# Both SwiGLUs of a decoder layer in two passes over their weights, with seven products of quarters for gate and linear

## The chip, the core and the metric

The kernel runs on one core of a Trainium2 chip. The metric is the device time of one launch in microseconds, from the first instruction to the last output. The engines are TensorE (PE, its weight loads PEld), VectorE (DVE), ScalarE (ACT), GpSimd (POOL) and SyncE (SP), which here only issues DMAs. Each engine takes its instructions in order.

## The reference, cut to what matters

One layer works on 1024 prompt tokens and 64 sample tokens (8 sequences of 8) with the same weights. Width is 1024, the SwiGLU's hidden width is 2816, all is float32.

```python
def swiglu(x, w_gu, w_down):
    g, u = jnp.split(x @ w_gu, 2, axis=-1)
    return (jax.nn.silu(g) * u) @ w_down

def layer(x, ...):
    h = x + 0.5 * rms_norm(swiglu(rms_norm(x, g_f1_pre), w_f1_gu, w_f1_down), g_f1_post)
    mix, k_new, v_new, s_new = mixer(rms_norm(h, g_m_pre), ...)   # attention and retention
    h = h + rms_norm(mix, g_m_post)
    h = h + 0.5 * rms_norm(swiglu(rms_norm(h, g_f2_pre), w_f2_gu, w_f2_down), g_f2_post)
    return h, k_new, v_new, s_new
```

## The kernel before

Activations stand transposed: features on the 128 partitions, tokens along the free axis. The 1088 tokens are three chunks, `CH = [(0, 384), (384, 384), (768, 320)]`.

Each float32 operand of a product is split into an upper part in fp32r (`hi`, L75, on ACT) and the rest (`lo`, L78, on DVE or POOL, source minus upper part, two SBUF tiles read). `mm3` (L85 to L92) makes a product from three matmuls: upper by upper (L87), upper by rest (L91), rest by upper (L92). Every matmul has a weight load of its own.

A SwiGLU (`ffn`, L317) walks over the 22 blocks f of 128 hidden columns, two at a time. For each f it loads the gate block and the linear block (8 tiles of 128x128 each, 512 KB) and the down block (512 KB), and splits each (`unit`: tiles wr, wh, wl, whd, wld). For each chunk, `gu` makes the gate product (8 `mm3`), a Silu on ACT (L337), the linear product (8 `mm3`), their product on DVE (L342, tile fs), and its two parts hh and hl. `down` (L349) multiplies these by the two down blocks for 8 blocks of output, and DVE adds each into the tile y (L359). So weights are read once and all tokens go by them; all 1088 tokens of a SwiGLU have ended before the boundary behind it is done.

A boundary (L283) is the post-norm, the residual and the next pre-norm: squares on ACT (L241) summed on DVE (L243), a small chain for the reciprocal root, then 8 steps with the gain (L294, one operand in PSUM), the residual from DRAM (xr, L296, half on POOL, half on DVE), the same squares again and L305. The three chunks take turns in `BOUNDARY_ORDER`. The layer starts with `first_norm` (L184), chunk by chunk among the first products, and ends with `stages_last`.

A scheduler sets each engine's order from program order and dependencies; pools give tiles with a number of buffers, and a tile's next user waits until its last reader is done. PSUM has two banks pa, two pb, three pc and one pm.

Of the kernel before, what the change touches and what calls it, by code (L numbers as in the profile page):

```python
# [2 lines left out]

# [14 lines left out]
P = 128  # L18
# [27 lines left out]
FIRST_HEAD = 7  # L46
BOUNDARY_ORDER = (0, 0, 1, 0, 1, 2, 1, 2, 2)


class Trunk:  # L50
# [11 lines left out]
    def pool(self, name, ctx=None, **kw):  # L62
        kw.setdefault("bufs", 1)
        return (ctx or self.ctx).enter_context(self.tc.tile_pool(name=name, **kw))
# [20 lines left out]
    def mm3(self, ps, wh, wl, xh, xl, first, last):  # L85
        mm = self.nc.tensor.matmul
        ins = mm(ps, wh, xh, start=first, stop=False)  # L87
        if self.pin is not None:
            self.behind(ins, self.pin)
            self.pin = None  # L90
        mm(ps, wh, xl, start=False, stop=False)  # L91
        mm(ps, wl, xh, start=False, stop=last)  # L92

    def unit(self, src, pool=None, sfx="", eng=None):
# [3 lines left out]
        raw = self.t(self.wraw, [P, 1024], "wr", bufs=2)  # L98
# [24 lines left out]
    def setup(self):  # L123
# [3 lines left out]
        self.wsp = self.pool("wsp", bufs=4)  # L127
        self.up = self.pool("up")
        self.gstage = self.pool("gst")
# [17 lines left out]
        self.mrT = self.t(self.dram, [D, T], "mrT")  # L147

# [9 lines left out]
    def rows_of_pages(self):  # L158
# [3 lines left out]
        t = self.t(self.gstage, [P, 384], "gs", bufs=3)  # L162
# [21 lines left out]
    def first_norm(self, pl, u, y, c):  # L184

        nc = self.nc
        co, cn = CH[c]
        out = self.bank("pb")
        dg = self.t(pl, [P, 3, P], "ndg", bufs=2)
        ss = self.t(pl, [P, 3], "ss", bufs=2)  # L190
        nc.gpsimd.memset(ss, 1.0)
        for j in range(3):
            o, n = TOK[3 * c + j]
            xn = self.t(pl, [P, D], "xn", bufs=3)
            nc.sync.dma_start(xn[:n], self.rows(3 * c + j))
            sq = self.t(pl, [P, D], "xsq")
            ins = nc.scalar.activation(sq[:n], xn[:n], AF.Square, accum_out=ss[:n, j : j + 1])
            if c == 1:
                self.behind(ins, self.first[1])
            for q in range(2):  # L200
                ps = self.bank("pc")
                for k in range(4):
                    ins = nc.tensor.transpose(ps[:, k * P : k * P + n],
                                              xn[:n, (4 * q + k) * P : (4 * q + k + 1) * P], self.ident[:n, :n])
                    if c == 1:
                        self.behind(ins, self.first[0])
                pv = ps.rearrange("p (k c) -> p k c", c=P)[:, :, :n]
                yv = y[:, 4 * q : 4 * q + 4, o - co : o - co + n]
                if c == 0:
                    nc.vector.tensor_copy(yv, pv)  # L210
                else:
                    nc.scalar.activation(yv, pv, AF.Copy)
        nc.vector.tensor_scalar(ss, ss, 1.0 / D, EPS, op0=ALU.mult, op1=ALU.add)
        nc.vector.reciprocal(ss, ss)
        nc.scalar.activation(ss, ss, AF.Sqrt)
        for j in range(3):
            o, n = TOK[3 * c + j]
            nc.vector.tensor_scalar(dg[:n, j, :n], self.ident[:n, :n], ss[:n, j : j + 1], None, op0=ALU.mult)
            ins = nc.tensor.matmul(out[:, o - co : o - co + n], self.ones[:n, :], dg[:n, j, :n], start=True, stop=True)
        if c == 0:  # L220
            self.first = [ins.ins]
            self.gains(["g_ffn1_pre"])
        g = self.gain["g_ffn1_pre"]
        for d in range(KD):
            v = self.t(pl, [P, 384], "nu", bufs=2)
# [1127 lines left out]
```

## Time and profile before

| | us |
|---|---|
| median of 3 runs | 3019.94 (3017.34 to 3020.51) |
| the profiled execution | 3022.61 |
| its span | 3020.7 |
| granted TensorE clock, mean | 0.989 |
| PE busy / DVE / ACT / POOL | 2943.9 / 1571.7 / 1066.9 / 305.7 |

A span is what the profile covers; the execution has 1.9 us around it. A matmul's busy time overlaps the next one's, so TensorE's load is read from distances between starts. Roughly, the first SwiGLU fills the span up to 800 us, its boundary follows until 900, the mixer reaches to about 2150, and the second SwiGLU to the end.

### The profile page before, as it was taken

Reading aid. Unit: us, or ns where it says so; the run is one execution under the profiler, and the core shown is the slowest. Engines: PE = TensorE matmul, PEld = TensorE weight load, DVE = VectorE, ACT = ScalarE, POOL = GpSimd, SP = SyncE. Lnnn points to the kernel's source line nnn. Section 1 sums busy time; section 2 is a strip of 40 time slices with the busy share of each in tenths; the row PEclk is TensorE's granted clock in tenths of the full one; section 3 lists DMA queues with packets and bytes.
Section 4 is the critical chain, followed back from the end, with each engine's and each line's share of the span. In section 5 each row is a group of like instructions: output and inputs, shape, how many; then the busy total and the mean of one; then the engine's idle time right before and its main releaser. Section 6 shows DMA issues by size and latency. Waiting matters only on the chain.

```text
span 3020.7 us, 44684 instructions
## 1 busy us (share of the span) xinstructions
PE 2943.9 (97%) x17944; PEld 2857.6 (95%) x17944; DVE 1571.7 (52%) x3034; ACT 1066.9 (35%) x2027; POOL 305.7 (10%) x339
## 2 busy tenths in 40 slices
PE   8999999999989999999999989999999999999998
PEld 7999999999989999989999878879999999999998
DVE  4333333333753554448888578876463333333336
ACT  5211111111443343336666577753342111111113
POOL 1000000000330000000000345430230000000001
PEclk9999999999999999999999999999999999999999
DMA  5211111111242332233223577767242111111112
GB/s 160 82 50 49 43 43 42 43 42 43 84 152 61 93 105 81 85 95 81 68 64 90 184 246 267 262 199 228 74 124 67 43 42 43 42 43 43 42 43 94
DMA packets 289200, 282.40 MB, mean 93 GB/s; under 512 B 25121, under 2 KB 263585, under 8 KB 288993
## 3 DMA queue, kind: packets, MB, share of 16 engines
q1 hardware_dynamic: 266720, 208.23, 22.4%
q0 software_dynamic: 22272, 71.31, 7.2%
q8 instruction: 141, 2.31, 0.3%
q14 instruction: 67, 0.54, 0.1%
HBM read 223.79 MB, written 51.51 MB: 91 GB/s over the span
## 4 chain that ended last, share of the span: by engine, by line
PE 61%; DVE 5%; DMA 2%; issue 1%; ACT 1%; POOL 0%; SPq 0%; DVEq 0%; ACTq 0%; POOLq 0%
PE pa L87 13%; PE pa L92 13%; PE pa L91 13%; PE pc L87 3%; PE pc L92 3%; PE pc L91 3%; PE pb L802 2%; PE pc L828 2%; PE pb L87 1%; PE pb L92 1%; PE pb L91 1%; DMA ul<-orT 1%; PE pm L631 1%; PE pm L855 1%; PE pm L856 1%
## 5 line engine op out<-in xcount | busy, mean ns | idle before, releaser
L87 PE MATMUL pa<-uh,wh 128*128 128x384 f32 (+1 forms) x3552 | 1171.8, 331 | 11.8 <-ACT gs L406 5.6
L92 PE MATMUL pa<-uh,wl 128*128 128x384 f32 (+1 forms) x3552 | 1166.8, 329 | 0.0
L91 PE MATMUL pa<-ul,wh 128*128 128x384 f32 (+1 forms) x3552 | 1165.8, 328 | 0.5 <-POOL ul L78 0.4
L87 PEld LDWEIGHTS pa<-uh,wh 128*128 128x128 f32 x3552 | 670.6, 189 | 23.5 <-ACT gs L406 6.7
L91 PEld LDWEIGHTS pa<-ul,wh 128*128 128x128 f32 x3552 | 670.4, 189 | 6.9 <-POOL ul L78 1.2
L92 PEld LDWEIGHTS pa<-uh,wl 128*128 128x128 f32 x3552 | 670.1, 189 | 3.0 <-issue 1.2
L359 DVE TENSOR_TENSOR y<-y,pc 128x384 f32<-128x384 f32 (+1 forms) x480 | 253.8, 531 | 417.7 <-PE pc L92 417.3
L91 PE MATMUL pc<-hl,whd 128*128 128x384 f32 (+1 forms) x1056 | 345.3, 327 | 0.8 <-DVE hl L78 0.8
L87 PE MATMUL pc<-hh,whd 128*128 128x384 f32 (+1 forms) x1056 | 342.9, 328 | 1.8 <-DVE y L359 1.7
L92 PE MATMUL pc<-hh,wld 128*128 128x384 f32 (+1 forms) x1056 | 342.1, 327 | 0.0
L78 DVE TENSOR_TENSOR wl<-wr,wh 128x1024 fp32r<-128x1024 f32 x144 | 176.2, 1224 | 212.6 <-ACT wh L75 198.9
L75 ACT ACTIVATE wh<-wr 128x1024 fp32r<-128x1024 f32 x156 | 165.4, 1060 | 291.9 <-PE pa L91 243.4
L342 DVE TENSOR_TENSOR fs<-fs,pa 128x384 f32<-128x384 f32 x132 | 69.9, 530 | 314.2 <-PE pa L92 312.3
L337 ACT ACTIVATE fs<-pa 128x384 f32<-128x384 f32 x132 | 61.8, 468 | 453.3 <-PE pa L92 453.2
L75 ACT ACTIVATE hh<-fs 128x384 fp32r<-128x384 f32 x132 | 66.2, 501 | 420.5 <-DVE fs L342 420.4
L87 PEld LDWEIGHTS pc<-hh,whd 128*128 128x128 f32 x1056 | 198.4, 188 | 2.4 <-DVE y L359 2.2
L91 PEld LDWEIGHTS pc<-hl,whd 128*128 128x128 f32 x1056 | 199.0, 188 | 1.2 <-DVE hl L78 1.2
L92 PEld LDWEIGHTS pc<-hh,wld 128*128 128x128 f32 x1056 | 198.9, 189 | 0.0
L296 POOL TENSOR_TENSOR y<-y,xr 128x384 f32<-128x384 f32 (+1 forms) x24 | 29.2, 1223 | 857.0 <-DVE y L294 839.7
L78 DVE TENSOR_TENSOR ktl<-pc,kth 128x512 fp32r<-128x512 f32 x128 | 86.4, 684 | 20.5 <-ACT kth L75 19.5
L669 DVE TENSOR_TENSOR_SCAN pt<-pt 128x129 f32<-128x129 f32 (+3 forms) x96 | 91.6, 956 | 6.5 <-ACT pt L660 2.0
L78 DVE TENSOR_TENSOR hl<-fs,hh 128x384 fp32r<-128x384 f32 x132 | 72.8, 552 | 35.8 <-ACT hh L75 35.6
(308 smaller groups left out, 3786.3 us busy)
## 6 DMA issues: line engine op xcount, KB each, us to landing
wr<-in_w_ffn_gu_dram SPq DMA_DIRECT2D x88, 512.0 KB
wr<-in_w_in_dram SPq DMA_DIRECT2D x52, 512.0 KB
wr<-in_w_ffn_down_dram SPq DMA_DIRECT2D x44, 512.0 KB
xn<-in_x_prompt_dram SPq DMA_DIRECT2D x8, 512.0 KB
s<-in_state_ret_dram SPq DMA_DIRECT2D x16, 256.0 KB
rgs<-grT SPq DMA_DIRECT2D x16, 256.0 KB
ut_ret_state_sample_dram<-s SPq DMA_DIRECT2D x16, 256.0 KB
orT<-oc SPq DMA_DIRECT2D x16, 256.0 KB
```

The lines of the kernel that those rows point to most:

```text
L75: return self.nc.scalar.activation(dst, src, AF.Copy)
L78: (eng or self.nc.vector).tensor_tensor(dst, src, hi.bitcast(F32), op=ALU.subtract)
L87: ins = mm(ps, wh, xh, start=first, stop=False)
L91: mm(ps, wh, xl, start=False, stop=False)
L92: mm(ps, wl, xh, start=False, stop=last)
L337: nc.scalar.activation(s[:, :n], pg[:, :n], AF.Silu)
L342: nc.vector.tensor_tensor(h[:, :n], s[:, :n], pu[:, :n], op=ALU.mult)
L359: nc.vector.tensor_tensor(y[c][:, d, :n], y[c][:, d, :n], ps[:, :n], op=ALU.add)
L631: ins = nc.tensor.matmul(po[:, lo:256], vs[:, j, :], ats[j // 4][x][:, j % 4, lo:256], start=(j == 0 and x == 0), stop=(j == last and x == 1))
L669: nc.vector.tensor_tensor_scan(rev, rev, rev, initial=1.0, op0=ALU.mult, op1=ALU.bypass)
L802: ins = nc.tensor.matmul(ps, qd[:, b2, m * P : (m + 1) * P], kt, start=(m == 0 and x == 0), stop=(m == 3 and x == 1))
L828: nc.tensor.transpose(tp[:, i * P : (i + 1) * P], kp[i // 2][:, (i % 2) * 512 + m * P : (i % 2) * 512 + (m + 1) * P], self.ident)
```

## The change

Tokens go through a SwiGLU in two passes, 512 in pass 0 and 576 in pass 1 (`PASSES` holds the start and half the width: 256 and 288). A pass reads all weights again. The products of a block f are a 2x2 scheme: the rows are gate and linear block, the inner dimension is halved (features 0 to 511 and 512 to 1023), the columns are the two halves of the pass's tokens. Seven products of quarters (4 `mm3` each, of 256 or 288 columns) take the place of eight, in Winograd's form of Strassen's scheme. For this the weights need four sums (POOL, L464, L465, L466, L471 of the kernel after) and seven splits of 512 (sh, sl) instead of two of 1024. The tokens' quarters need four sums per block of features (`sums`), which are made once a pass. The results take three additions on DVE with a PSUM operand, two on POOL (L507, L508), and products accumulate in a PSUM bank that ACT has meanwhile read out.

```diff
+PASSES = ((0, 256), (512, 288))
+B11, B21, B22, T1, T2, T3, T4 = range(7)
+USED = (B11, T2, T3, T1, B21, T4, B22)
...
+    def sums(self, pl, q11, q12, q21, q22, emit, eng=None):
+        tt = (eng or self.nc.gpsimd).tensor_tensor
...
+        emit(B11, q11)
+        tt(t1, q12, q11, op=ALU.subtract)
+        tt(t2, q22, t1, op=ALU.subtract)
+        emit(T2, t2)
+        tt(q12, q22, q12, op=ALU.subtract)
+        emit(T3, q12)
+        emit(T1, t1)
+        emit(B21, q21)
+        tt(t4, q21, t2, op=ALU.subtract)
+        emit(T4, t4)
+        emit(B22, q22)
...
+    def late_quarters(self, u):
+        for b in USED:
+            lf = u[1][b].bitcast(F32)
+            self.nc.sync.dma_start(lf, self.cB[:, b])
+            self.hi(u[0][b], lf)
+            self.lo(u[1][b], lf, u[0][b])
...
+    def swiglu_weights(self, wgu, f):
...
+        names = ("A11", "S2", "S3", "S1", "A12", "A22", "S4")
+        out = {x: [self.t(self.sw, [P, 512], y, F32R, bufs=9) for y in ("sh", "sl")] for x in names}
...
+        tt = nc.gpsimd.tensor_tensor
+        split("A11", g0)
+        split("A22", v1)
+        tt(v1, v0, v1, op=ALU.add)
+        tt(v0, g0, v0, op=ALU.subtract)
+        tt(g0, v1, g0, op=ALU.subtract)
+        split("S2", g0)
+        split("S3", v0)
+        split("S1", v1)
+        split("A12", g1)
+        tt(g1, g1, g0, op=ALU.subtract)
+        split("S4", g1)
+        return out
+
+    def swiglu_hidden(self, w, u, n):
...
+        px = self.bank("pa")
+        product(px, "A11", B11)
+        p1 = kept("p1", px)
+        py = self.bank("pb")
+        product(py, "S2", T2)
+        u2 = self.t(fs, [P, 288], "u2", bufs=2)[:, :n]
+        tt(u2, py[:, :n], p1, op=ALU.add)
+        pw = self.bank("pa")
+        product(pw, "S3", T3)
+        p7 = kept("p7", pw)
+        pz = self.bank("pb")
+        product(pz, "S1", T1)
+        p5 = kept("p5", pz)
+        nc.gpsimd.tensor_tensor(p7, p7, p5, op=ALU.add)
+        nc.gpsimd.tensor_tensor(p7, p7, u2, op=ALU.add)
+        product(px, "A12", B21, True)
+        nc.scalar.activation(h1, px[:, :n], AF.Silu)
+        product(pw, "A22", T4, True)
+        c21 = self.t(fs, [P, 288], "c21")[:, :n]
+        tt(c21, pw[:, :n], u2, op=ALU.add)
+        tt(h1, h1, c21, op=ALU.mult)
+        product(pz, "S4", B22, True)
+        tt(h2, pz[:, :n], u2, op=ALU.add)
+        nc.scalar.activation(h2, h2, AF.Silu)
+        tt(h2, h2, p7, op=ALU.mult)
...
+            for p, (o, n) in enumerate(PASSES):
+                for g in range(0, NF, 2):
+                    hid = [self.swiglu_hidden(self.swiglu_weights(wgu, f), q, n) for f in (g, g + 1)]
...
+                    if g + 2 == NF and p == 0:
+                        q = self.new_quarters(self.qpool, PASSES[1][1])
+                        self.late_quarters(q)
+                    down(p, g, dw, hid)
+                    side(p, g // 2)
...
-                for c, (o, n) in enumerate(CH):
+                for c, (o, n) in enumerate(mch):
```

In `down`, a chunk is 512 wide in pass 0; in pass 1 it is 256 and 320 (first SwiGLU) or 320 and 256 (second). What lies around the SwiGLUs moves too. `first_norm` now covers the first 512 tokens; the others are normed beside pass 0 (`second_norm`), and their quarters go to DRAM (cB) and come back between the passes (`late_quarters`). The boundary of pass 0's tokens runs beside pass 1, in halves of 256; behind the first SwiGLU only 576 tokens are left (256 and 320), and the normed first 512 come back from DRAM (unT). The output products of the mixer go in chunks of 512, 288 and 288 (`mch`); the first 512 tokens' boundary and quarters come before the second SwiGLU, the others' beside its pass 0. Pools of SBUF get `reuse_waits="tile"`.

Three places in the engines' order follow. In the kernel after, `hi` is L88, `lo` L91, `mm3` L100 to L105, and the addition into y L570.

TensorE in the middle of the first SwiGLU before: the down products (pc) of a pair stand between the gate and linear products (pa) of the next.

```order
L92 MATMUL pc_2568<-hh_2402,wld_2175 128x384
L87 MATMUL pa_2749<-uh_13_92,wh_2720 128x384
L91 MATMUL pa_2749<-ul_16_95,wh_2720 128x384
L92 MATMUL pa_2749<-uh_13_92,wl_2721 128x384
L87 MATMUL pa_2749<-uh_13_92,wh_2720 128x384
L87 MATMUL pc_2576<-hh_2231,whd_2168 128x384
L91 MATMUL pc_2576<-hl_2232,whd_2168 128x384
L92 MATMUL pc_2576<-hh_2231,wld_2169 128x384
```

TensorE in pass 0 after, at the same place: pa_1578 is A22's product, pb_1709 the next f's S2, pb_1593 S4's product.

```order
L105 MATMUL pa_1578<-q_22_107,sl_1526 128x256
L100 MATMUL pb_1709<-q_18_103,sh_1663 128x256
L100 MATMUL pc_1454<-hh_1268,whd_1420 128x512
L104 MATMUL pc_1454<-hl_1269,whd_1420 128x512
L105 MATMUL pc_1454<-hh_1268,wld_1421 128x512
L100 MATMUL pc_1454<-hh_1414,whd_1426 128x512
L104 MATMUL pc_1454<-hl_1415,whd_1426 128x512
L105 MATMUL pc_1454<-hh_1414,wld_1427 128x512
L100 MATMUL pb_1593<-q_23_108,sh_1527 128x256
```

The down products stand between quarters' products of 12 matmuls as before, now 512 wide, and a product of the next f can be begun ahead.

POOL before, from the end of the start to the first SwiGLU's boundary: nothing stands between the last lower part of the start and the first residual.

```order
L78 TENSOR_TENSOR ul_18_97<-nu_725,uh_15_94 128x320
L78 TENSOR_TENSOR ul_18_97<-nu_729,uh_15_94 128x320
L296 TENSOR_TENSOR y_19_110<-y_19_110,xr_6746 128x384
L296 TENSOR_TENSOR y_19_110<-y_19_110,xr_6755 128x384
L296 TENSOR_TENSOR y_19_110<-y_19_110,xr_6764 128x384
```

POOL after, for one f in pass 0: wr are the raw weights, p and u the kept results.

```order
L464 TENSOR_TENSOR wr_444_2282<-wr_444_2282 128x512
L465 TENSOR_TENSOR wr_444_2282<-wr_2281,wr_444_2282 128x512
L466 TENSOR_TENSOR wr_2281<-wr_444_2282,wr_2281 128x512
L507 TENSOR_TENSOR p_420_2122<-p_420_2122,p_422_2137 128x256
L508 TENSOR_TENSOR p_420_2122<-p_420_2122,u_418_2107 128x256
L471 TENSOR_TENSOR wr_2281<-wr_2281 128x512
```

Six sums for each f are new on POOL, all from SBUF.

DVE before, in the same SwiGLU: additions into y, with one product and one lower part of the hidden block among them.

```order
L359 TENSOR_TENSOR y_20_114<-y_20_114,pc_4318 128x384
L342 TENSOR_TENSOR fs_4484<-fs_4484,pa_4459 128x384
L359 TENSOR_TENSOR y_20_114<-y_20_114,pc_4326 128x384
L78 TENSOR_TENSOR hl_4512<-fs_4484,hh_4511 128x384
L359 TENSOR_TENSOR y_20_114<-y_20_114,pc_4334 128x384
```

DVE after, in pass 0: sl are lower parts of the quarters of the next f, hf the hidden block.

```order
L515 TENSOR_TENSOR c_350_1781<-pa_1724,u_345_1722 128x256
L516 TENSOR_TENSOR hf_1693<-hf_1693,c_350_1781 128x256
L91 TENSOR_TENSOR sl_1913<-wr_1896,sh_1912 128x512
L91 TENSOR_TENSOR sl_2047<-wr_2042,sh_2046 128x512
L519 TENSOR_TENSOR hf_1693<-pb_1739,u_345_1722 128x256
L91 TENSOR_TENSOR sl_2057<-wr_399_2043,sh_2056 128x512
L521 TENSOR_TENSOR hf_1693<-hf_1693,p_347_1737 128x256
L91 TENSOR_TENSOR hl_1800<-hf_1693,hh_1799 128x512
L499 TENSOR_TENSOR u_390_1961<-pb_1948,p_388_1946 128x256
L91 TENSOR_TENSOR sl_2049<-wr_2042,sh_2048 128x512
```

Between the steps of the hidden block now stand lower parts of weights; the next f's A11 (sl_2047) and A22 (sl_2057) come before S2 (sl_2049), which needs POOL's three sums.

580 lines of the change are left out of this document (364 added, 216 removed).

## The prediction

> **What bounds the kernel now.** I read the page's busy line and chain first, then the stages, then the shapes of each engine, then single rows where two engines meet.
>
> ```profile
> span 3020.7 us, 44684 instructions
> PE 2943.9 (97%) x17944; PEld 2857.6 (95%) x17944; DVE 1571.7 (52%) x3034; ACT 1066.9 (35%) x2027; POOL 305.7 (10%) x339
> PE 61%; DVE 5%; DMA 2%; issue 1%; ACT 1%; POOL 0%; SPq 0%; DVEq 0%; ACTq 0%; POOLq 0%
> ```
>
> TensorE carries the chain. The stages (the columns are the window, its length, busy time of PE, PEld, DVE, ACT and POOL with counts, granted clock, DMA share, GB/s) show where it does not:
>
> ```profile
> 0.00:75.00 75.00, 62.35 (x340) 59.69 (x341) 37.52 (x76) 42.97 (x71) 9.44 (x19) 0.91 0.53 159
> 300.00:500.00 200.00, 200.00 (x1213) 200.00 (x1212) 71.28 (x117) 31.73 (x49) 0.00 (x0) 1.00 0.14 43
> 800.00:850.00 50.00, 43.02 (x254) 41.46 (x253) 42.04 (x87) 25.66 (x51) 22.12 (x16) 0.92 0.49 158
> 850.00:900.00 50.00, 44.49 (x236) 42.64 (x236) 22.80 (x43) 21.96 (x40) 20.11 (x24) 0.87 0.40 127
> 3000.00:3021.00 21.00, 10.38 (x64) 8.64 (x63) 11.81 (x25) 8.78 (x19) 2.87 (x2) 0.81 0.61 217
> ```
>
> In the middle of a SwiGLU TensorE never rests, DVE is busy 36%, ACT 16%, POOL not at all: time there is the sum of the spacings of matmuls. A row's own duration (0.28 to 0.40 us) overlaps the next, so I take start to start. First and last of a run, the columns being start and duration: 24 of 320 columns, 51 of 384, twelve of 256, three of 512.
>
> ```profile
> 409.44 0.31 PE L87 MATMUL pa<-uh,wh 128*128 128x320 f32 x1
> 412.81 0.31 PE L92 MATMUL pa<-uh,wl 128*128 128x320 f32 x1
> ...
> 413.31 0.34 PE L87 MATMUL pa<-uh,wh 128*128 128x384 f32 x1
> 421.98 0.33 PE L92 MATMUL pa<-uh,wl 128*128 128x384 f32 x1
> ...
> 971.96 0.28 PE L91 MATMUL pb<-rscl,rvh 128*128 128x256 f32 x1
> 973.27 0.28 PE L92 MATMUL pm<-rvh,kdl 128*128 128x256 f32 x1
> ...
> 2006.33 0.40 PE L856 MATMUL pm<-vl,at 128*128 128x512 f32 x1
> 2006.79 0.46 PE L856 MATMUL pm<-vl,at 128*128 128x512 f32 x1
> ```
>
> That gives 0.1465, 0.1734, 0.119 and 0.23 us. 288 columns lie halfway between 256 and 320: 0.1328. Check: a mix of two 384s and one 320 is 0.1644, and 200 us over 1213 is 0.1649.
>
> **The change: TensorE.** I count by pair of column blocks f, which is the kernel's unit (11 pairs in a SwiGLU). Before, a pair has 144 matmuls for each of three chunks: 288 x 0.1734 + 144 x 0.1465 = 71.0 us. After, pass 0 has 2 x 84 at 256 and 48 down matmuls at 512: 20.0 + 11.0 = 31.0. Pass 1 has 168 at 288 and 48 each at 256 and 320: 22.3 + 12.7 = 35.0. So 66.1 against 71.0, 4.95 less for a pair, 109 us for 22 pairs. One eighth of the gate and linear products goes, but narrower matmuls give back half of it, since their fixed part is some 0.01 us each. The Trainium skill (TensorE: Matmul & The Clock Gate, "Wait — 56ns, not 53.3ns?") puts spacing at columns over 2.4 GHz plus 2.5 ns; estimated by that the saving would be 117, and the rows, with a larger fixed part, contradict it.
>
> **What stands beside it: DVE and POOL.** These engines now split seven weight quarters for each f and pass instead of two blocks once, and POOL makes four sums of weights and two of results. Durations:
>
> ```profile
> L78 DVE TENSOR_TENSOR wl<-wr,wh 128x1024 fp32r<-128x1024 f32 x144 | 176.2, 1224 | 212.6 <-ACT wh L75 198.9 <-PE pc L1051 13.5
> L78 DVE TENSOR_TENSOR ktl<-pc,kth 128x512 fp32r<-128x512 f32 x128 | 86.4, 684 | 20.5 <-ACT kth L75 19.5
> L243 DVE TENSOR_TENSOR acc<-acc,sq 128x256 f32<-128x256 f32 x16 | 6.6, 415 | 0.1
> L75 ACT ACTIVATE vh<-wl 128x512 fp32r<-128x512 f32 x64 | 39.7, 627 | 21.1 <-PE pm L855 13.3 <-DMA wl<-in_cache_v_dram,rowix 2.8 <-DVE pt L748 2.0
> ...
> 809.06 0.55 DVE L243 TENSOR_TENSOR accb<-accb,sqb 128x384 f32<-128x384 f32 x1
> 809.53 0.54 DVE L359 TENSOR_TENSOR y<-y,pc 128x384 f32<-128x384 f32 x1
> ...
> 822.83 8.22 POOL L78 TENSOR_TENSOR ul<-y,uh 128x384 fp32r<-128x384 f32 x8 [5.60 <-ACT uh L75]
> ```
>
> Back to back, DVE instructions start 0.08 us sooner than the one before ends (0.47 for 0.55), so one of 1024 costs 1.14, of 512 0.60, of 256 0.335; by the line through these, of 288 0.37 and of 576 0.67. A pair of pass 0 needs 14 lower parts of 512, two of the hidden block, two of down weights, four products from SBUF (13.2 us), and six evacuations of 256 and eight additions of 512 into y (6.8): 20.0 us of 31.0. Pass 1: 13.5 + 8.1 = 21.6 of 35.0. ACT has 16 of 512, two of 1024 (twice that) and ten of 256 (at most half): about 16 us. POOL takes 1.03 us for 384 and 2.36 for 1024 (below), so 1.30 for 512, 0.76 for 256, 0.83 for 288: 13.4 us a pair in pass 0, 13.7 in pass 1. Taken singly, all are hidden under TensorE. Together they are not free:
>
> ```profile
> 795.99 2.81 POOL L78 TENSOR_TENSOR wl<-wr,wh 128x1024 fp32r<-128x1024 f32 x1
> ...
> 796.45 0.55 DVE L359 TENSOR_TENSOR y<-y,pc 128x384 f32<-128x384 f32 x1
> 796.92 2.31 DVE L296 TENSOR_TENSOR y<-y,xr 128x384 f32<-128x384 f32 x1
> ...
> 814.87 2.36 POOL L78 TENSOR_TENSOR wl<-wr,wh 128x1024 fp32r<-128x1024 f32 x1 [3.00 <-ACT wh L75]
> ...
> 815.36 2.21 DVE L78 TENSOR_TENSOR hl<-fs,hh 128x320 fp32r<-128x320 f32 x1 [0.26 <-ACT hh L75]
> ```
>
> A DVE instruction that reads two SBUF tiles (hl, y with xr) lasts until POOL's has ended, 2.2 us instead of 0.5, while one with a PSUM operand beside the same POOL instruction keeps its 0.55. The Trainium skill (SBUF — State Buffer, "Who interferes with whom") says just this, an exclusive lock on a shared read port. By its rule 13.2 + 13.4 = 26.6 us of a 31.0 us pair hold the lock, which alone would stall nothing.
>
> But both engines take their instructions in order, and one chain has little slack. When TensorE has used S1 of the pair's second f, the slot for the next f's A22 is free. Then follow ACT's upper part (0.6), DVE's lower part, three POOL sums one after another, ACT and DVE again for S2: 0.6 + 0.6 + 3.9 + 0.6 + 0.6 = 6.3, with six handovers some 6.9 us. TensorE's order gives it three products, the next A11 and about nine down matmuls: 48 x 0.119 + 9 x 0.23 = 7.8 us. With the lock, two DVE instructions of 0.6 slip between the POOL sums and one DVE part waits for half a sum (0.65): 8.8. The slot opens once a pair, so I add 1.3 us a pair, rounded up for the additions into y that queue behind a blocked part: 44 pairs, +57 us. The ends: 0, if collisions fall into slack, and 176 us (second rival). Gaps of 1 us cost no clock as yet; a longer one does:
>
> ```profile
> 33.71 0.69 PE L87 MATMUL pa<-uh,wh 128*128 128x384 f32 x1 [2.47 <-ACT fs L337]
> 34.20 0.52 PE L91 MATMUL pa<-ul,wh 128*128 128x384 f32 x1
> 34.52 0.52 PE L92 MATMUL pa<-uh,wl 128*128 128x384 f32 x1
> ```
>
> After 2.47 us of idleness the spacing is 0.32 instead of 0.17.
>
> Added weight loads (66 of 512 KB in a SwiGLU) double a DMA share of 0.14; SP issues them in program order, between the boundaries' loads and spills, and each has a 15 us f to land in. I add nothing; without that cover a late load would stop the chain above at its first split.
>
> **The seams.** Start: the second 256 tokens need 16 POOL sums (12.2 us) beside six of weights (7.8) before all quarters stand, while TensorE has two f's products with B11 and B21 to do; the window from 0 to 75 loses 12.7 us as it is. +5 (-5 to +15). End of the first SwiGLU: 800 to 900 loses 12.5 us idle and some 9 to the clock; 512 of 1088 tokens now go through it under pass 1: -8 (-18 to +5). Into the second SwiGLU: 512 tokens' norms (36 additions and 32 gains of 256, some 25 us of DVE), their quarters (5 + 9) and a pair's weights (8) make 48 on DVE, two thirds of POOL's 16 on top, 59, against 16 x 24 x 0.1328 = 51 us of output products: +8, and +4 for the two norm chains: +12 (0 to +30). Between passes the late quarters are seven splits of 1152 (1.27 each, 9 us) on a DVE two thirds full: +4 twice (0 to +16). Tail: -3 (-8 to +3). The mixer's own work is the same. Sum +14, ends about -10 and +45.
>
> **Sum.** The profiled execution took 3022.6 us, the span and 1.9 around it, 2.7 above the median of 3019.9. 3022.6 - 109 + 57 + 14 = 2984.6; against the median, 2982.
>
> **Rivals.**
> First, all hidden: the lock's collisions stay in slack. For it: 26.6 of 31.0, and two products of lead in the weight slots (nine, seven used). Against: the chain above. Time: 2982 - 57 = 2925, with good seams 2905.
> Second, slower: DVE becomes the bound. If every microsecond of POOL stops it, a pair of pass 0 takes 33.4 and one of pass 1 35.3; the work beside (second norm, 23 us of DVE and POOL over 11 pairs; boundaries with quarters, 40; boundaries of pass 1, 29) adds 2.1, 3.6 and 2.4. That is 5.3 over TensorE in pass 0 and 2.7 in pass 1, 176 us: 3101, with partial overlap some 3060. Against: a third of DVE's time reads PSUM and passes. It decides from (109 - 14) / 44 = 2.2 us a pair.
> Third, the change does not save TensorE time: weight loads bind at 256 columns. Their mean is 189 ns, above the 119 spacing:
>
> ```profile
> L87 PEld LDWEIGHTS pa<-uh,wh 128*128 128x128 f32 x3552 | 670.6, 189 | 23.5 <-ACT gs L406 6.7 <-ACT fs L337 3.8 <-ACT qdec L540 2.7
> ```
>
> But the 256-column run above has a load for each matmul and kept 0.119, so loads overlap. At 0.146 as for 320, pass 0 and pass 1 would lose 22 x (168 x 0.027 + 168 x 0.0137) = 150 us, and the time be 3130.
>
> **How the numbers follow.** Forecast 0.45, its own range 2940 to 3015; hidden 0.25; DVE bound 0.26; no saving 0.04. Within 0.2% (6 us, about what a measurement of this kernel can tell from no change) lies the forecast's upper edge: 0.07. Faster: 0.25 and most of 0.45, 0.66. Slower: 0.27. The range of eight in ten reaches from the hidden case with good seams, 2905, into the DVE case, 3070.
>
> **What will show it.** Right: 256- and 288-column matmuls at 0.119 and 0.133 start to start; POOL at some 13 us a pair; lower parts of 512 with a mean of 0.8 to 1.0 us where undisturbed ones take 0.68; TensorE idle about 1 us a pair, released by ACT or DVE with S2's parts. Wrong: idle before down matmuls released by DVE's additions into y, or a granted clock below 0.95 in the SwiGLUs (DVE bound); TensorE without gaps (hidden); spacing above 0.13 at 256 (no saving). The seams may also cost more than 30 us where output products run out.

## The result and the profile after

| | us | against the kernel before, same chip |
|---|---|---|
| before, median of 4 runs | 3020.2 (3017.3 to 3022.3) | |
| after, median of 4 runs | 3043.5 (3041.2 to 3050.7) | 1.0082 (1.0063 to 1.0101) |
| forecast | 2982 (2905 to 3070) | |

The changed kernel is 0.8% slower, a small step but clear of the spread of the runs. The time lies in the forecast's range, on the other side of the kernel before.

The page of the kernel after, its span, the busy line and the chain of work:

```profile
span 3042.1 us, 50675 instructions
...
PE 2875.8 (95%) x19002; PEld 2715.4 (89%) x19002; DVE 2212.6 (73%) x4059; ACT 1480.9 (49%) x2953; POOL 1004.9 (33%) x879
...
PE 16%; DVE 5%; POOL 2%; issue 2%; DMA 1%; ACT 1%; SPq 0%; POOLq 0%; DVEq 0%; ACTq 0%
```

The shares of the chain (16% for TensorE, 61% before) cannot be compared: they are shares of the whole span, and here the chain could be followed back only to 2242 us, before to 888. What changed is read from the stages. Those of the kernel after (columns as in the prediction: the window, its length, PE, PEld, DVE, ACT and POOL with counts, granted clock, DMA share, GB/s) follow:

```profile
0.00:75.00 75.00, 48.13 (x244) 42.13 (x245) 55.11 (x97) 43.71 (x99) 33.35 (x41) 0.91 0.57 152
150.00:240.00 90.00, 90.00 (x635) 83.92 (x634) 73.40 (x113) 46.66 (x90) 45.51 (x34) 1.00 0.45 137
400.00:530.00 130.00, 118.45 (x816) 111.58 (x815) 123.59 (x221) 71.84 (x139) 61.12 (x48) 0.99 0.44 133
600.00:760.00 160.00, 160.00 (x1206) 160.00 (x1205) 116.19 (x205) 65.82 (x124) 71.14 (x54) 1.00 0.29 87
800.00:850.00 50.00, 39.97 (x233) 38.24 (x232) 38.84 (x73) 29.65 (x53) 17.07 (x14) 0.87 0.52 155
850.00:900.00 50.00, 40.82 (x223) 39.46 (x223) 21.81 (x44) 19.73 (x35) 15.37 (x20) 0.85 0.42 133
2200.00:2275.00 75.00, 52.90 (x346) 49.05 (x346) 61.51 (x131) 39.51 (x96) 33.13 (x21) 0.84 0.40 120
```

The second and the fourth row are pairs with no other work beside them, in pass 0 and pass 1: TensorE rests nowhere, though DVE is busy 82% and 73%. The others are the start, the change of passes with the first boundary beside it (DVE 95%), the end of the first SwiGLU, and the way into the second. Two runs of products in clean pairs of the kernel after, 33 matmuls of 256 columns and twelve of 288 (start and duration, first and last of each):

```profile
159.79 0.28 PE L100 MATMUL pa<-q,sh 128*128 128x256 f32 x1
163.56 0.27 PE L105 MATMUL pa<-q,sl 128*128 128x256 f32 x1
...
650.13 0.29 PE L100 MATMUL pa<-q,sh 128*128 128x288 f32 x1
651.60 0.29 PE L105 MATMUL pa<-q,sl 128*128 128x288 f32 x1
```

3.77 us over 32 is 0.118, 1.47 over 11 is 0.1336: the spacings of the forecast. So I can work out for every stage what TensorE lost beyond its spacing: the distances between neighbouring starts, each less the spacing of its width (0.119, 0.1328, 0.1465, 0.1734 and 0.23 us; 0.11 for narrower ones). Stages are the first 100 us; from there to the last down product of the first SwiGLU; the 80 us behind it; the mixer; the two output products; 60 us behind them; the rest of the second SwiGLU; the last 5 us of down products and all that follows. Each kernel's profiled execution, in us:

| | start | first SwiGLU | behind it | mixer | output products | into the second | second SwiGLU | tail | sum |
|---|---|---|---|---|---|---|---|---|---|
| before | 18.6 | 8.0 | 18.0 | 89.9 | 5.3 | 2.8 | 1.5 | 5.5 | 149.6 |
| after | 41.0 | 37.2 | 21.6 | 95.3 | 9.5 | 31.7 | 32.4 | 8.9 | 277.6 |
| difference | +22.4 | +29.2 | +3.6 | +5.4 | +4.2 | +28.9 | +30.9 | +3.4 | +128.0 |

Span less loss is TensorE's own work: 2871.1 before, 2764.5 after, 106.6 less where the forecast had 109. The saving is all there; 128 us of new waiting ate it. Of the 60 us that the two SwiGLUs lose more, some 53 stand at 240 to 300 us (7.9, second norm's last part), 400 to 530 (19.1), 2300 to 2400 (12.6, the boundary beside pass 0) and 2575 to 2700 (14.1), all with work beside the pair, and most of the rest at 3000 to 3013, where the last pair ends. The clean pairs of the table's second and fourth row lose 0.3 and 0.1 us.

What holds TensorE up on the way into the second SwiGLU (the two longest waits of PE in 2200 to 2275: in total, times, longest):

```profile
PE pm L382 <- DVE acc L371: 5.8, 1, 5.8
PE pb L100 <- ACT sh L88: 5.3, 1, 5.3
```

Inside that gap stand these instructions of DVE and POOL (start, duration):

```profile
2223.64 0.68 DVE L91 TENSOR_TENSOR sl<-wr,sh 128x512 fp32r<-128x512 f32 x1
...
2224.45 6.52 POOL L464 TENSOR_TENSOR wr<-wr 128x512 f32<-128x512 f32 x1 [20.99 <-DVE sl L91]
...
2224.91 1.21 DVE L91 TENSOR_TENSOR wld<-wrd,whd 128x1024 fp32r<-128x1024 f32 x1
...
2227.05 0.45 DVE L371 TENSOR_TENSOR acc<-acc,sq 128x288 f32<-128x288 f32 x1
...
2231.05 1.26 POOL L465 TENSOR_TENSOR wr<-wr,wr 128x512 f32<-128x512 f32 x1
```

The first sum of weights, 1.26 us of work by the row below it, takes 6.52 on POOL: DVE streams instructions with two SBUF operands without a break until 2229.8, and POOL gets through only behind them. S2 (a sum of weight quarters) waits for that sum and the two behind it, and TensorE for S2: the 5.3 us. The 5.8 us before are a small matmul of the boundary of the last 576 tokens, whose sum of squares (2227.05) stands in the same stream of DVE. At the change of passes the hold goes the other way (DVE's groups in 400 to 530: busy, mean ns, idle before):

```profile
L371 DVE TENSOR_TENSOR acc<-acc,sq 128x256 f32<-128x256 f32 x28 | 21.3, 762 | 0.4
...
L91 DVE TENSOR_TENSOR q<-q,q 128x1152 fp32r<-128x1152 f32 x5 | 9.6, 1929 | 0.0
```

A sum of squares of 256 takes 0.76 us, undisturbed 0.42. All 28 sums of the boundary stand in these 130 us, just where the late quarters are split.

### The profile page after: what moved, and what is told of

Read it like the earlier page. It is cut to its first block, busy times and chain, and to the rows that moved or that the text cites. A ratio compares the mean times of both kernels' runs of the same rounds, so it can differ in the third digit from the quotient of the medians.

```text
span 3042.1 us, 50675 instructions
## 1 busy us (share of the span) xinstructions
PE 2875.8 (95%) x19002; PEld 2715.4 (89%) x19002; DVE 2212.6 (73%) x4059; ACT 1480.9 (49%) x2953; POOL 1004.9 (33%) x879
## 5 line engine op out<-in xcount | busy, mean ns | idle before, releaser
L88 ACT ACTIVATE sh<-wr 128x512 fp32r<-128x512 f32 x616 | 351.8, 622 | 411.3 <-POOL wr L471 192.8
L91 DVE TENSOR_TENSOR sl<-wr,sh 128x512 fp32r<-128x512 f32 x616 | 443.3, 746 | 116.5 <-ACT sh L88 115.0
L100 PE MATMUL pa<-uh,wh 128*128 128x384 f32 (+1 forms) x1440 | 483.4, 336 | 7.5 <-ACT gs L598 2.5
L105 PE MATMUL pa<-uh,wl 128*128 128x384 f32 (+1 forms) x1440 | 477.0, 331 | 0.0
L104 PE MATMUL pa<-ul,wh 128*128 128x384 f32 (+1 forms) x1440 | 476.7, 331 | 0.0
L100 PE MATMUL pa<-q,sh 128*128 128x256 f32 (+1 forms) x1408 | 411.2, 292 | 11.0 <-DVE c L515 5.4
L104 PE MATMUL pa<-q,sh 128*128 128x256 f32 (+1 forms) x1408 | 411.3, 292 | 6.0 <-DVE q L91 5.9
L105 PE MATMUL pa<-q,sl 128*128 128x256 f32 (+1 forms) x1408 | 409.4, 291 | 0.7 <-DVE sl L91 0.7
L100 PE MATMUL pc<-hh,whd 128*128 128x256 f32 (+2 forms) x1056 | 329.2, 333 | 19.7 <-ACT hh L88 14.7
L105 PE MATMUL pc<-hh,wld 128*128 128x256 f32 (+2 forms) x1056 | 344.2, 329 | 0.0
L100 PE MATMUL pb<-q,sh 128*128 128x288 f32 (+1 forms) x1056 | 308.4, 293 | 16.5 <-ACT sh L88 9.5
L104 PE MATMUL pb<-q,sh 128*128 128x288 f32 (+1 forms) x1056 | 309.2, 293 | 5.5 <-DVE q L91 5.5
L570 DVE TENSOR_TENSOR y<-y,pc 128x512 f32<-128x512 f32 (+2 forms) x480 | 243.9, 525 | 89.9 <-PE pc L105 88.2
L105 PE MATMUL pb<-q,sl 128*128 128x288 f32 (+1 forms) x1056 | 308.1, 292 | 0.4 <-DVE sl L91 0.3
L100 PEld LDWEIGHTS pa<-uh,wh 128*128 128x128 f32 x1440 | 274.4, 191 | 18.2 <-ACT uh L88 2.9
L100 PEld LDWEIGHTS pa<-q,sh 128*128 128x128 f32 x1408 | 269.1, 191 | 18.0 <-DVE c L515 6.4
L104 PEld LDWEIGHTS pa<-q,sh 128*128 128x128 f32 x1408 | 268.8, 191 | 11.2 <-DVE q L91 8.4
L105 PEld LDWEIGHTS pa<-uh,wl 128*128 128x128 f32 x1440 | 273.8, 190 | 2.9 <-issue 1.2
L105 PEld LDWEIGHTS pa<-q,sl 128*128 128x128 f32 x1408 | 268.6, 191 | 2.6 <-DVE sl L91 0.9
L464 POOL TENSOR_TENSOR wr<-wr 128x512 f32<-128x512 f32 x88 | 129.2, 1468 | 359.2 <-DVE sl L91 343.0
```

What stands on the lines that cost most here:

```text
L88: return self.nc.scalar.activation(dst, src, AF.Copy)
L91: (eng or self.nc.vector).tensor_tensor(dst, src, hi.bitcast(F32), op=ALU.subtract)
L464: tt(v1, v0, v1, op=ALU.add)
L570: nc.vector.tensor_tensor(y[p][:, d, c], y[p][:, d, c], ps[:, :n], op=ALU.add)
```

## The experiments

Theory: TensorE's new waits lie where other work stands beside the pairs, because DVE is full there, and it is full for two reasons: POOL's sums hold it up (and it them), and the side work is crowded into short stretches. Rivals: plain load (DVE would be full without POOL's help at any order), the boundaries alone, the layout in two passes. Each ratio is against runs of the kernel before on the same chip.

**Sums on DVE** (the edit at the weights; `sums` and the two sums of results likewise).

```diff
-        tt = nc.gpsimd.tensor_tensor
+        tt = nc.vector.tensor_tensor
```

> All sums of weights, of results and of the tokens' quarters go from POOL to DVE (the splits stay where they are). Theory of the lock: the 130 us that TensorE loses beyond its spacing in the stretches with side work (start, 240 to 300 us, both pass changes, into the second SwiGLU) come from DVE and POOL holding each other up; a POOL sum of 512 takes 1.3 to 1.45 us and now and then 3 to 6, DVE does it in 0.60. So TensorE's idle time falls in all these stretches, start -8 to -10, into the second SwiGLU -10 to -15, each pass change -6, 2300 to 2400 -8: 2990 to 3005 us, DVE's lower parts of 512 back to a mean of 0.69. Rival, plain load: DVE is simply full there, and POOL carries 6.2 us a pair for it at a cost of 3.4 us of stretching; then the clean passes stay hidden (26 of 31 and 28 of 35 us), but the 15 or so pairs with side work lose 2.8 us more each and the start 8: about 3090 us.

Measured: 3022.3 us, 0.9996 (0.9985 to 1.0006): 21 us faster than after, about half of what the theory of the lock said, and far from 3090. The page, two groups of it, and three windows:

```profile
PE 2865.4 (95%) x19002; PEld 2713.3 (90%) x19002; DVE 2304.1 (76%) x4635; ACT 1486.7 (49%) x2953; POOL 260.1 (9%) x303
```

```profile
L91 DVE TENSOR_TENSOR sl<-wr,sh 128x512 fp32r<-128x512 f32 x616 | 404.1, 685 | 33.0 <-ACT sh L88 31.2
L464 DVE TENSOR_TENSOR wr<-wr 128x512 f32<-128x512 f32 x88 | 60.5, 687 | 0.2
```

```profile
0.00:75.00 75.00, 48.43 (x291) 44.20 (x292) 60.51 (x144) 47.95 (x107) 1.06 (x11) 0.82 0.61 163
400.00:530.00 130.00, 125.27 (x898) 122.76 (x898) 123.15 (x270) 72.22 (x142) 8.04 (x8) 0.97 0.44 130
2200.00:2275.00 75.00, 53.35 (x356) 49.56 (x355) 71.75 (x170) 45.18 (x103) 3.51 (x4) 0.82 0.44 133
```

745 us of POOL's busy time are gone and DVE has 92 more: the sums take some 290 us there (0.69 each for 512 columns), but DVE's other work takes some 200 less. Which instructions got shorter tells why. These are two groups of the kernel after and the same two of this run:

```profile
L516 DVE TENSOR_TENSOR hf<-hf,c 128x256 f32<-128x256 f32 (+1 forms) x88 | 69.9, 794 | 4.9 <-ACT hf L511 0.7
L515 DVE TENSOR_TENSOR c<-pa,u 128x256 f32<-128x256 f32 (+1 forms) x88 | 38.0, 431 | 17.1 <-PE pa L105 17.0
...
L516 DVE TENSOR_TENSOR hf<-hf,c 128x256 f32<-128x256 f32 (+1 forms) x88 | 39.4, 447 | 1.5 <-ACT hf L511 0.6
L515 DVE TENSOR_TENSOR c<-pa,u 128x256 f32<-128x256 f32 (+1 forms) x88 | 38.2, 434 | 9.5 <-PE pa L105 9.1
```

The product of two SBUF tiles goes from 794 to 447 ns and the lower parts of weights from 746 to 685; the addition of the same width with an operand in PSUM stays as it was (431 and 434). The start loses 33.2 in place of 41.0, the change of passes 9.3 in place of 19.1; the way into the second SwiGLU hardly changes (29.0 for 31.7), and DVE is still 95% busy in both of the later windows. So the lock was one cause, and not the only one.

**Side work in fine steps**, alone and with the sums on DVE.

```diff
+                        tick(p, g // 2)       # behind each block of down products: one step
...
-                    next(todo["ends"][BOUNDARY_ORDER[g - 1]], None)
+        todo["t1", 1] = ticker([fine(0, o, 256, ...) for o in (0, 256)], 1, 3)
```

> The work beside the passes (second norm, boundaries, quarters, last boundary of the first 512 tokens) is cut into steps of one or two DVE instructions and handed out one at a time behind each block of down products (every one in pass 0, every third in pass 1), in place of lumps of 8 to 15 us once a pair. Sums stay on POOL. Theory that lumps cause the loss inside the passes: 240 to 300 (7.9 us), 2300 to 2400 (12.5) and two thirds of the pass changes (19 and 14) go: about -35, 3005 to 3015 us, with the start and the way into the second SwiGLU unchanged. Rival, DVE has too little time for side work at any spacing (21 us of pair plus 3.5 of stretching plus side work): 3035 to 3050.

> Both edits together: sums on DVE and side work in fine steps. If lock and lumps are separate causes, the gains add, 2955 to 2975 us, faster than the kernel before. If spreading works only because it keeps DVE from being full for long, sums on DVE give part of it back: 2985 to 3005. If plain load rules: above 3040.

Measured: 3039.3 us, 1.0055 (1.0042 to 1.0069), and 3025.3 us, 1.0005 (0.9996 to 1.0014): next to nothing by itself, nothing on top of the sums. DVE's sums of squares in 400 to 530 of the run with sums on POOL show why:

```profile
L457 DVE TENSOR_TENSOR acc<-acc,sq 128x256 f32<-128x256 f32 x28 | 20.5, 732 | 0.2
```

All 28 still stand in that window, though the program now hands them out over eight pairs. The order is the scheduler's, which put the finer steps back to the same place. For the boundaries this run tested nothing of the theory; the order had to be pinned. Only at 240 to 300 us, beside the second norm, did the loss fall, from 7.9 to 0.8 us.

**Boundaries beside the passes left out.**

```diff
-                todo["ends"] = [first_boundary(0, o, 256, kept, ("pm", "pm")) for o in (0, 256)]
+                todo["ends"] = [self.bare(y[0][:, :, o : o + 256], o, 256, self.h1T, kept) for o in (0, 256)]
```

> Left out: the boundary of the first 512 tokens beside pass 1 of the first SwiGLU and that of the last 576 beside pass 0 of the second (only their copies to DRAM stay). That takes some 42 and 47 us of DVE off the stretches 400 to 530 and 2260 to 2400. Theory that the boundaries fill DVE there: TensorE's loss falls from 19 to about 8 at the first pass change and from 12.5 to 1 in 2300 to 2400, some of the 7 us behind the start of the second SwiGLU too: -25 to -30, 3013 to 3018 us. Rival, late quarters are what TensorE waits for at the pass change: only -12 to -15, 3030.

Measured: 3009.0 us, 0.9951 (0.9937 to 0.9964), 34 less than after, a little more than the theory's 25 to 30. The window of the change of passes:

```profile
400.00:530.00 130.00, 127.97 (x924) 125.04 (x925) 104.68 (x164) 56.96 (x107) 61.26 (x45) 1.00 0.41 126
```

TensorE loses 3.5 us there in place of 19.1, with the late quarters still in it, and 0.4 in place of 12.6 at 2300 to 2400. It is the boundary, or rather its meeting with the late quarters, not the quarters alone.

**Output products in smaller chunks** (with the sums on DVE).

```diff
-        mch = [(0, 512), (512, 288), (800, 288)]
+        mch = [(0, 256), (256, 256), (512, 288), (800, 288)]
```

> Sums on DVE as in the first run, and the mixer's output products in chunks of 256, 256, 288, 288 in place of 512, 288, 288: the first half of the first 512 tokens is done some 22 us sooner. Theory of the chain: TensorE's 30 us of loss on the way into the second SwiGLU come from two post-norms and two pre-norms one after another (squares, root, gains, residuals) that begin too late, with DVE only half busy: beginning 22 us sooner takes 12 to 18 us off, 3004 to 3010 us. Rival: the amount of DVE work just ahead of the first products (quarters, 28 lower parts, weights of two f) sets it: 0 to 4 us off, 3018 to 3022.

Measured: 3035.0 us, 1.0037 (1.0024 to 1.0050), 13 slower than with the sums on DVE alone. Both theories are wrong here, the first most. The longest wait of PE in 2180 to 2300, and from the same trace what stands before S2:

```profile
PE pb L100 <- ACT sh L88: 15.2, 2, 12.6
```

```profile
2232.14 0.68 DVE L464 TENSOR_TENSOR wr<-wr 128x512 f32<-128x512 f32 x1
2233.08 3.47 DVE L422 SCALAR_TENSOR_TENSOR y<-y,g_mix_post,pm 128x288 f32<-128x288 f32 x8
...
2239.56 0.67 DVE L466 TENSOR_TENSOR wr<-wr,wr 128x512 f32<-128x512 f32 x1
2242.30 0.44 ACT L369 ACTIVATE acc<-y 128x288 f32<-128x288 f32 x1 [3.68 <-POOL y L424]
2242.64 2.18 ACT L88 ACTIVATE sh<-wr 128x512 fp32r<-128x512 f32 x4
```

The output products lost 18.6 us in place of 10.1, and TensorE still stood 12.6 us before S2. Beginning the norms sooner did not bring the first pair's weights forward: between the first (L464) and the last (L466) of the three sums, 8.1 us, DVE has eight gains of the next tokens' boundary (3.47 us), quarters and down weights, and then S2's upper part stands 2.4 us behind a square on ACT that waits for that boundary's residual on POOL. Why the output products lose 8.5 us more stays open.

**Seven slots in place of nine for weight quarters.**

```diff
-        out = {x: [self.t(self.sw, [P, 512], y, F32R, bufs=9) for y in ("sh", "sl")] for x in names}
+        out = {x: [self.t(self.sw, [P, 512], y, F32R, bufs=7) for y in ("sh", "sl")] for x in names}
```

> Slots for weight quarters cut from nine to seven, so that A22 of the next f can only be split when TensorE has used this f's A22. Theory: the two slots of lead are what hid the chain that the prediction charged with 1.3 us a pair; without them the chain (8 to 9 us) has only S4's and A11's products beside it (2.9 us) at every f that no down products follow, 4 to 6 us of idle time at each of 44 places: 3220 to 3300 us. Rival, TensorE's order finds other work: within 20 us of 3043.

Measured: 3042.4 us, 1.0063 (1.0042 to 1.0083): as after. My reading of the slots fell. From the trace, the time between the end of a quarter's lower part on DVE and the first product that reads it, in clean pairs of pass 1 (600 to 760 us), median of nine f (A22 is a quarter as loaded; S2, S3 and S1 are made by POOL's three sums):

| | A22 | S2 | S3 | S1 |
|---|---|---|---|---|
| after | 27.5 | 9.8 | 13.6 | 14.0 |
| seven slots | 24.8 | 5.7 | 9.0 | 12.3 |

A22 is split more than 20 us ahead of its product either way, while by a strict turn of seven slots it could not be split before this f's A22 had been used, 12 to 21 us ahead of the next. The slots are thus not handed out in the fixed turn on which the prediction's chain rested. The addresses of the tiles in the built program show the turn: in the kernel after, the lower part of A22 takes over the slot of S4 of two f before in 75 of 88 cases, not that of S1 of the f before. In the trace (600 to 760 us) its split on DVE starts 1 to 4 us after that slot's last use, so it does wait for a slot, but for one that comes free early.

**Eight products in the same two passes.**

```diff
-USED = (B11, T2, T3, T1, B21, T4, B22)
+USED = (B11, B21, B12, B22)
...
-        names = ("A11", "S2", "S3", "S1", "A12", "A22", "S4")
+        names = ("A11", "A12", "A21", "A22")
```

> The two passes without Strassen's scheme: eight products of quarters of the same widths, weights split into four quarters of 512, no sums of weights, tokens or results. TensorE's work by the spacings is 133 us more than with seven, 24 more than in the kernel before. Theory that seven splits and the sums cause what TensorE lost inside the passes and at the pass changes, and the layout causes the rest (later start, way into the second SwiGLU, mixer): 3085 to 3105 us, seven products thus worth only some 50 of 133. Rival, the two-pass layout loses all of the 130 us: 3170.

Measured: 3067.2 us, 1.0145 (1.0124 to 1.0166), less than both said. TensorE's work is 2897 us, 132 more than after, but it loses 168.2, only 19 more than the kernel before. Windows as for after:

```profile
0.00:75.00 75.00, 55.96 (x375) 52.30 (x376) 40.70 (x93) 39.00 (x81) 1.07 (x11) 0.91 0.66 183
400.00:530.00 130.00, 130.00 (x958) 128.16 (x958) 88.05 (x188) 54.72 (x97) 8.76 (x8) 1.00 0.44 131
2200.00:2275.00 75.00, 67.31 (x485) 64.98 (x484) 49.19 (x120) 35.98 (x79) 11.82 (x8) 0.95 0.49 145
```

The layout in two passes, with boundaries beside them and late quarters, costs TensorE little waiting, 4.1 and 1.4 us inside the SwiGLUs; its narrower matmuls add 26 us of work (2897 against 2871). What seven products add on DVE and POOL costs 109 of the 132 us that they save.

**Side work pinned**, with weight sums and the start's sums on DVE, and then with all sums on POOL (in both, the first steps of the second norm stay at one a pair).

```diff
+    def late(self, ins):
+        if self.mark is not None:
+            self.behind(ins, self.mark)       # mark: the addition into y at which the step is handed out
+        return ins
...
-            nc.scalar.activation(sq[:, :n], src[:, d, :n], AF.Square)
+            self.late(nc.scalar.activation(sq[:, :n], src[:, d, :n], AF.Square))
```

> As in the run with fine steps, but each step's instructions are held in the engines' order behind the addition into y at which they are handed out, since without that the scheduler put both boundaries back into 400 to 530 us. Weight sums and the start's sums on DVE; sums of results and of the tokens' quarters for DRAM stay on POOL. Theory that DVE is only full because the side work stands together: losses at 240 to 300, 400 to 530, 2300 to 2400 and 2575 to 2700 us fall from 54 in all to 15 to 20, with the gain of the start from the first run: 2985 to 3000 us. Rival, DVE lacks the time at any spacing: 3015 to 3030.

> The order edit alone: side work in fine steps held behind the additions into y, all sums on POOL as in the kernel after. Theory that the time at which side work stands is the cause inside the passes: some 40 of the 54 us lost at 240 to 300, 400 to 530, 2300 to 2400 and 2575 to 2700 go, start (41) and the way into the second SwiGLU (32) stay: 3000 to 3010 us. Rival, POOL's hold on DVE is needed for the loss as much as the order (spread over all pairs, 3.5 us of stretching and 5 to 7 of side work on top of 20 to 22 fill 31 us): 3020 to 3030.

Measured: 2985.6 us, 0.9871 (0.9850 to 0.9893), and 3013.4 us, 0.9970 (0.9960 to 0.9980). The change of passes in the first of them, its sums of squares there, and the same window in the second:

```profile
400.00:530.00 130.00, 130.00 (x961) 128.73 (x960) 115.03 (x215) 62.78 (x118) 19.05 (x17) 1.00 0.36 107
```

```profile
L466 DVE TENSOR_TENSOR acc<-acc,sq 128x256 f32<-128x256 f32 x7 | 2.9, 420 | 0.2
```

```profile
400.00:530.00 130.00, 127.61 (x928) 125.42 (x929) 107.12 (x181) 60.02 (x115) 59.84 (x48) 1.00 0.32 95
```

Seven sums of squares in place of 28, and TensorE does not rest. The order alone took 30 us off the kernel after, the sums alone 21, both together 58. They are two causes and about add up (30 and 21 against 58). The mix also leaves the sums of results and the quarters for DRAM on POOL; what that is worth by itself was not measured.

**The second boundary one pair later**, on top of the pinned mix, and **the first pair with eight products** on top of that.

```diff
-                                     self.h2T, lambda *x: None) for o in (512, 800)] + [to_dram(j) for j in range(4)], 0, 1)
+                                     self.h2T, lambda *x: None) for o in (512, 800)] + [to_dram(j) for j in range(4)], 1, 1)
...
+                    pl8 = p == 0 and g == 0
+                    hid = [self.swiglu_hidden(self.swiglu_weights(wgu, f, pl8), q, n, pl8) for f in (g, g + 1)]
+                    if pl8:
+                        first()               # the token sums, behind the first pair's products
```

> As the pinned run with weight sums on DVE, but the boundary beside pass 0 of the second SwiGLU begins behind the second pair in place of the first. Theory: in the first pair TensorE stood 5.8 us behind a small matmul of that boundary, which waited for DVE's sum of squares while DVE was full with the first weights: 4 to 7 us less, 2979 to 2982 us. Rival: TensorE would have waited for weights there anyway: 2985.

> On top of that, the first pair of each SwiGLU is made with eight products (four weight quarters and four token quarters, no sums), the token sums following behind it. TensorE has 2.9 us more work in each SwiGLU. Theory: what the start (36 us lost, 19.8 with eight products throughout) and the way into the second SwiGLU (32 against 11) lose is the time for sums and for seven splits ahead of the first products; then 12 to 16 and 8 to 12 us go, less 6: 2960 to 2970 us. Rival, the sums are only put off and stop the second pair: within 4 us of the run beside it.

Measured: 2980.8 us, 0.9864 (0.9849 to 0.9880), and 2959.5 us, 0.9793 (0.9780 to 0.9807). The first step is 5 us by the medians and 0.07% (2 us) by the ratios, as the two runs were made on different chips, and the intervals of the ratios overlap: the time doesn't settle it. In the trace the way into the second SwiGLU loses 19.7 us in place of 25.0, which fits the theory. The second step, on the same chip as the first, is 21 us faster again and 2.1% faster than the kernel before; windows of this run:

```profile
0.00:75.00 75.00, 52.76 (x347) 50.55 (x348) 51.45 (x126) 46.43 (x100) 2.54 (x13) 0.93 0.62 163
400.00:530.00 130.00, 130.00 (x976) 129.50 (x976) 115.54 (x217) 63.92 (x120) 22.57 (x20) 1.00 0.37 110
2200.00:2275.00 75.00, 75.00 (x535) 70.56 (x534) 69.90 (x130) 41.92 (x84) 10.21 (x11) 1.00 0.38 116
```

**Each sum before S2 twice on POOL.**

```diff
+        dum = self.t(self.fw, [P, 512], "dum")
+        tt(dum, v0, v1, op=ALU.add)           # and so before each of the three sums
         tt(v1, v0, v1, op=ALU.add)
```

> The kernel after, with the three sums between A22's and S2's splits each made twice on POOL (once into a spare tile), which lengthens by some 4 us per f the chain that the prediction charged with 1.3 us a pair. In the trace of after S2's parts stand ready 8.5 to 12 us ahead of their product in clean pairs, since A22 is split 27 us ahead of its own. Theory of the lead: in clean pairs (150 to 240, 600 to 760 us) TensorE still loses nothing and S2 is ready about 5 us ahead; only the stretches that are full already lose more: 3055 to 3080 us. Rival, the prediction's chain with 7.8 us of cover: another 4 us at each of 44 places, 3200 us or more.

Measured: 3199.0 us, 1.0578 (1.0560 to 1.0595): the rival's number, not mine. Two windows without side work, and DVE's lower parts in the second:

```profile
150.00:240.00 90.00, 84.46 (x565) 76.02 (x564) 69.87 (x99) 40.66 (x79) 58.81 (x47) 1.00 0.37 102
600.00:760.00 160.00, 154.01 (x1127) 151.69 (x1126) 127.97 (x192) 63.02 (x120) 108.41 (x80) 0.99 0.29 87
```

```profile
L91 DVE TENSOR_TENSOR sl<-wr,sh 128x512 fp32r<-128x512 f32 x62 | 57.8, 956 | 12.9 <-ACT sh L88 12.9
```

Clean pairs now lose 8.3 us in 90 and 10.2 in 160, 2 to 3 a pair. In pass 0 the parts of S2, S3 and S1 come down to 0.1 to 0.4 us ahead of their products, where after had at least 3.6, 8.1 and 8.4: the chain binds. In pass 1 S2 is still 6.8 us ahead, and TensorE waits for additions into y and for the hidden block instead, DVE's lower parts being stretched to 0.96 us. So the stalls that the prediction described do exist, one doubling away; the kernel after has just enough lead not to show them in clean pairs. The rival's time came out in part by luck: its mechanism, S2 late by the chain, is seen in the window of pass 0, while in that of pass 1 TensorE waits for other things.

The losses of the runs that matter, as in the table above:

| | start | first SwiGLU | behind it | mixer | output products | into the second | second SwiGLU | tail | sum |
|---|---|---|---|---|---|---|---|---|---|
| after | 41.0 | 37.2 | 21.6 | 95.3 | 9.5 | 31.7 | 32.4 | 8.9 | 277.6 |
| sums on DVE | 33.2 | 31.2 | 26.2 | 92.7 | 10.1 | 29.0 | 27.1 | 8.7 | 258.2 |
| pinned, sums on POOL | 38.4 | 20.1 | 24.5 | 92.8 | 8.9 | 28.1 | 21.7 | 9.3 | 243.8 |
| pinned, weight sums on DVE | 35.6 | 11.8 | 23.4 | 96.0 | 9.8 | 25.0 | 9.9 | 8.5 | 220.0 |
| and the boundary later | 35.4 | 11.6 | 23.2 | 92.8 | 9.5 | 19.7 | 11.7 | 8.7 | 212.6 |
| and the first pair plain | 26.0 | 12.4 | 23.7 | 90.5 | 9.1 | 4.1 | 8.6 | 10.4 | 184.8 |
| eight products | 19.8 | 4.1 | 20.5 | 93.1 | 8.8 | 11.2 | 1.4 | 9.3 | 168.2 |

## Why the prediction was wrong

- **TensorE, -109: right.** 106.6 measured, spacings of 0.118 and 0.1336. The rival that weight loads bind at 256 columns is out.
- **The stall of +57: wrong mechanism, and a size that fits by luck.** With the change of passes, the SwiGLUs lose 60 us more than before (29.2 and 30.9); the forecast had 57 and 8. By its own terms it is further off: some 33 of the 60 stand at the two changes of passes, forecast at 8, so 27 are left for the pairs, and none of them in clean pairs. The step that failed is "the slot opens once a pair": A22 takes a slot that comes free earlier than S1's, is split 27 us ahead of its product, and S2 stands ready 9.8 us early. The loss comes from some 415 us with side work, where DVE is busy 88 to 95%. So the first rival (all hidden) holds in the clean pairs, and the second (DVE as the bound) in the stretches; its working spread the side work over 11 pairs, while the scheduler put a whole boundary into some four of them.
- **DVE's load was put too low.** The prediction added up 20.0 us a pair in pass 0 and 21.6 in pass 1. The clean windows show DVE busy 82% and 73%, which is 25.3 and 25.4 us a pair. Some 3.4 of that is the stretching beside POOL's sums: five groups of the pair (lower parts of weights, of down weights and of the hidden block, and its two products) lose 148 us over 44 pairs when the sums leave POOL. The load left little room for side work.
- **The seams, +14: the term that decided the sign.** Without the change of passes the forecast had +6, the trace shows +68: start +22.4 (forecast +5), behind the first SwiGLU +3.6 (-8), mixer and output products +9.6 (0), into the second SwiGLU +28.9 (+12), tail +3.4 (-3). 62 us more than forecast, and 2982 plus 62 is 3044. The start came out above its upper end (+15) and the way in just under its own (+30), together with the changes of passes, which the range of the sum (-10 to +45) did not allow for. The step that failed here is the comparison of amounts (for the way in, 59 us of DVE's work against 51 us of output products), as if all of that work could stand beside the products. With eight products in the same two passes the start loses 19.8 us in place of 41.0 and the way in 11.2 in place of 31.7, so most of both terms is what seven products add: sums of tokens and weights and seven splits, one behind the other ahead of the first products. The run that makes only the first pair with eight products takes the way in from 19.7 to 4.1 us and the start from 35.4 to 26.0. POOL's hold is the smaller part: moving its sums to DVE took 7.8 us off the start and only 2.7 off the way in, although one sum lasted 6.52 us there.
- **The sums on POOL were counted as help.** 745 us of POOL's time stood for 92 us of DVE's. The Trainium skill (Perfetto Trace Analysis, "Optimizing Scalar/DVE Operations") warns that moving work between these two engines might not help since they share a read port; the run with the sums on DVE agrees, 3022 against 3043 us. The rule that the Trainium skill states elsewhere (SBUF — State Buffer, "Who interferes with whom"), that whoever issues first holds the port and the other is fully blocked, fits the 2.21 us of DVE that the prediction shows. Of POOL's 6.52 us it fits the wait behind one instruction; that POOL waits through a whole row of DVE's instructions, not just one, is what the 6.52 us add to it.
- **A slip in the sum of the second rival:** 29 us over 11 pairs is 2.6 a pair, not 2.4, which adds 5 us to its 176 and changes no choice.
- **What stays open:** why smaller output chunks made the output products themselves slower, what makes up the rest of DVE's load above the count, and some 9 us of small losses in the mixer and the output products, whose order shifted with the rest.

## What to carry to other kernels

A saving on the bounding engine is worth what the stages without cover leave of it. Price it per stage: steady pairs, each stretch with side work, each seam, and ask of every stretch which engine has no time left; here 107 us saved on TensorE met 128 us of waiting, most of it in stretches where DVE was busy 88 to 95% and at the seams, where sums and splits had to come before the first products. Before handing elementwise sums to POOL, look for rows in which it and DVE lengthen each other: work between two SBUF tiles may be cheaper on DVE, even when DVE is the fuller engine. And when side work is spread in the program, look in the engines' order whether it stayed spread; here nearly the same steps gave next to nothing until they were pinned, and 0.9% then (3039 to 3013 us).

## What the runs showed of the hardware

- A sum of two SBUF tiles of 128x512 takes 0.69 us on DVE, and on POOL a mean of 1.44 to 1.52 us by the groups of the kernel after, once 6.52 while DVE ran instructions with two SBUF operands back to back.
- Taking 745 us of such work off POOL lengthened DVE's busy time by only 92, since DVE's instructions with two SBUF operands got shorter (616 lower parts from a mean of 746 to 685 ns, products of the hidden block from 794 to 447), while those with an operand in PSUM kept 431 to 434 ns.
- The granted clock stayed at 1.00 in every clean window and fell to 0.84 to 0.87 in the windows of 50 to 75 us at 800, 850 and 2200 us, each of which has two gaps of 2.6 to 6.1 us, so a gap costs more than its length: of the 31.8 us that the kernel after lost in 2200 to 2275, 24.5 are in starts more than 0.3 us late, the other 7.3 in matmuls that followed each other slowly.
